# One hybrid decoder step in fp32: the first head's sampled states loaded and used later, and the recurrence's chunks spread differently among the fills

## The chip, the cores and the metric

The kernel runs on one core of a Trainium2 chip. The metric is the device time of the whole launch in microseconds. The kernel before took 1075.98 us as the median of three runs (1078.3, 1072.61 and 1075.98). The engines are named as in the profile: PE (TensorE, matmuls; PEld its weight loads), ACT (ScalarE), DVE (VectorE), POOL (GpSimd) and SP (SyncE), which here issues most of the DMA transfers.

## The reference, cut to what matters

One decoder layer works on 512 prompt tokens and 8 sampled tokens (520 rows in all, width 1024). Two branches start from the same normalised input and the same input projection `w_in`:

```python
s, o = lax.scan(chunk, s0, (split(q), split(k), split(v)))      # retention: 4 heads, key 256, value 512
o = o * lax.rsqrt(jnp.mean(o * o, axis=-1, keepdims=True) + NORM_EPS)
return o * jax.nn.silu(g_a.astype(f32)), s                      # gated by g_a
...
o, s = _rwkv_scan(r, w, k, v, kk, a, s0.astype(f32))            # RWKV-7: 16 heads of 64, a recurrence over tokens
```

Branch A's output (2048 wide) goes through `w_down_a`, branch B's (1024 wide) through `w_down_b`; both are multiplied by merge gates from `w_in` (called MA and MB below), added, and go through `w_out`, a per-layer embedding and a final norm. Prompt tokens start from a zero retention state. Each of the 8 sampled tokens has a state of its own (`state_ret`, 4 heads of 256 x 512 for each token), which is decayed, gets the outer product of the token's key and value added, is multiplied by the query and is written back.

## The kernel before, in words

Each fp32 matmul is made as three fp32r products. `weights` (L144) fetches a block of 1024 x 128 weights into `raw` (SP, L142; three buffers), copies it on ACT to `whi` (L147; two buffers) and takes `wlo = raw - whi` on DVE (L148; two buffers). `mm_half` (L152) then multiplies whi by the high part of the tokens, whi by their low part, and wlo by the high part, for one half of the tokens (256 or 264), into a PSUM bank of tag "h" (four banks). A tile of 1024 x 128 weights is 48 matmuls, a `w_down_a` tile 96.

The program is emitted in one order and then put in order engine by engine by a scheduler that has a time line of its own. What bends it are priorities (`tc.high_priority`), `tc.issue_after(x)`, which lets what follows be placed only behind instruction x, and dependencies added by hand (`after(i, prior)`, L195, a real wait). `tail` holds the last matmul of the last half, `marks` the last weight block's load, subtraction and copy. [...]

The stages: norms and startup; RWKV projections; then the four retention heads. A head makes k and q (L801 to L815), V in four quarters of the weights, j = 0 to 3, into four "h" banks (`phv`, L838; `vsm`, L831, makes the sampled tokens' V from the raw weights), the masked scores (L863 to L868), `sampled(h)` (L748) and four gate tiles (L891, whose sampled part L892 copies to `gs8`). `sampled(h)` loads the head's states in four transfers of 1 MB (POOL, L758; tile tS, four buffers), scales them on ACT (L764, 16 instructions of 512 columns), broadcasts the values (vb, L762), adds on DVE (L765), multiplies with the query (po, L770) and stores them (L774).

Then comes the RWKV recurrence in 8 chunks of 64 tokens. `chunk(c)` (L1017) starts with 64 small matmuls UO (L1025), then copies R, 32 matmuls U (L1034), copies SV, 32 dS (L1040), 32 UO (L1043), and ACT and DVE evacuate (Ot, L1056). Between the parts of a chunk the other engines must answer, and the PE works on fills meanwhile: 8 gate tiles of MB (`gate`, L212; ACT evacuates `mg`, L215) and 8 tiles of `w_down_a` (`down_a`, L1070), in which also the retention outputs are reloaded and split (yalo, yahi; L646). The table AT (L1100) says how many fills have been emitted ahead of each chunk.

Finished rows of the recurrence are stored to DRAM (YBd). Behind the recurrence they are loaded back (yb, L1149, by SP) and split (ybhi on ACT, L1150; yblo on DVE, L1151) for `w_down_b` (`proj`, L152 to L168). The transposes of x and of the embedding (xn, xt, pn, pt; L1157 on) and the loads of MBd and UAd (mb, ma) are placed about there too.

Of the kernel before, what the change touches and what calls it, by code (L numbers as in the profile page):

```python
# [8 lines left out]
F32 = mybir.dt.float32  # L9
F32R = mybir.dt.float32r  # L10
I32 = mybir.dt.int32
AF = mybir.ActivationFunctionType
# [5 lines left out]
T, B8, NT = 512, 8, 520  # L18
# [7 lines left out]
DV = 512  # L26
# [53 lines left out]
def body(tc, A, O, dbg=None, upto="Z"):  # L80
# [3 lines left out]
    act, dve, pe, sp, pool = nc.scalar, nc.vector, nc.tensor, nc.sync, nc.gpsimd  # L84
# [7 lines left out]
    with es:  # L92
# [5 lines left out]
        gs8 = cross.tile([128, 16, B8], F32, tag="gs8", name="gs8")  # L98
# [37 lines left out]
        tail = []  # L136
# [582 lines left out]
        def advance(kind=None):  # L719
            nonlocal due  # L720
            due += LOAD[kind] / UNITS * (WORK + 2 * WAIT) if kind else 2 * WORK
            with tc.issue_after(marks[1]):
                while due > 0:
                    w_ = next(extra, None)
                    if w_ is None:
                        break
                    due -= w_ + 60
# [17 lines left out]
        dve.tensor_tensor(s8, s8, i4[:, 2], ALU.add)  # L745
        dve.tensor_tensor(sum8, s8, i4[:, 3], ALU.add)

        def sampled(h):  # L748
            qz = pR.tile([128, 2, 4, 34], F32, tag="qz", name="qz", bufs=1)
            dve.memset(qz, 0.0)  # L750
            dve.tensor_copy(qz[:, :, :, 0], qs[:, h, :, 0:4])
            dve.tensor_copy(qz[:, :, :, 33], qs[:, h, :, 4:8])
            po = pq.tile([128, 512], F32, tag="po", name="po")
            for g in range(2):
                Ss = []
                for i in range(2):
                    S = pT.tile([128, 4, NT], F32, tag="tS", name="tS", bufs=4)[:, :, 0:DV]
                    pool.dma_start(S, A["state_ret"][0, 4 * g:4 * g + 4, h, 128 * i:128 * i + 128, :].rearrange("b p v -> p b v"))  # L758
                    Ss.append(S)
                for b in range(4):  # L760
                    vb = bank("vb")
                    pe.matmul(vb, sel[:, 4 * g + b, :], vsr, start=True, stop=True)  # L762
                    for i, S in enumerate(Ss):
                        act.activation(S[:, b, :], S[:, b, :], AF.Copy, scale=GAM[h])  # L764
                        last = dve.scalar_tensor_tensor(S[:, b, :], vb, ks[:, h, i, 4 * g + b:4 * g + b + 1], S[:, b, :], ALU.mult, ALU.add)  # L765

                for i, S in enumerate(Ss):
                    n_ = 32 if g == 0 and i == 0 else 2
                    for b in range(4):
                        m_ = pe.matmul(po[32 * b:32 * b + n_, :], qz[:, i, b, 32 * g:32 * g + n_], S[:, b, :],  # L770
                                       start=(n_ == 32), stop=(g == 1 and i == 1), skip_group_check=True)
                        if b == 0 and i == 0:
                            after(m_, last)
                    pool.dma_start(O[5][0, 4 * g:4 * g + 4, h, 128 * i:128 * i + 128, :].rearrange("b p v -> p b v"), S)  # L774
            return po

        def sampled_out(h, po):
# [6 lines left out]
            for i in range(4):  # L784
# [3 lines left out]
                              ps.rearrange("p (i b r) -> p i b r", i=4, b=4)[:, :, :, 0:2],  # L788
                              gs8[:, hs_, :].rearrange("p i (g b) -> p i b g", g=2), ALU.mult)

        OFF = [0, 512, 896, 1152]
        GBC = [0, 0, 0, 4, 8]
        for h in range(H):
# [33 lines left out]
            for j in range(4):  # L827
                ready = fetch(w_in[256 * j:256 * j + 256, O_V + DV * h:O_V + DV * h + DV])
                raws, w = raws[-1:] + [wide(ready[0])], [wide(t) for t in weights(None, ready=ready)]
                if j % 2:  # L830
                    ms = [pe.matmul(vsm[32 * g:32 * g + 32], hst[:, 2 * j - 2 + g, :], raws[g // 2][:, g % 2, :],  # L831
                                    start=(j == 1), stop=(j == 3), skip_group_check=True) for g in range(4)]
                    side_by_side(ms)
                    after(ms[0], marks[2])
                for jt in range(4):
                    for k in range(2):
                        for x, (w_, r) in enumerate(((w[0], hhi), (w[0], hlo), (w[1], hhi))):
                            m_ = pe.matmul(vps[jt], r[:, 2 * j + k, 128 * jt:128 * jt + 128], w_[:, k, :],  # L838
                                           start=(j == 0 and k == 0 and x == 0), stop=(j == 3 and k == 1 and x == 2))
                tail[:] = [getattr(m_, "ins", m_)]  # L840
                advance("v")
            vhi = pB.tile([128, 4, DV], F32R, tag="vhi", name="vhi")
            vlo = pB.tile([128, 4, DV], F32R, tag="vlo", name="vlo")
# [35 lines left out]
            for jt in range(4):  # L879
# [2 lines left out]
                    pe.transpose(ps[:, 128 * i:128 * i + 128], kf[i][:, 128 * jt:128 * jt + 128], ident)  # L882
                act.activation(dhi[:, jt, :], ps[:, 0:256], AF.Copy, scale=kdec[:, h, jt:jt + 1])
                dve.scalar_tensor_tensor(dlo[:, jt, :], ps[:, 0:256], kdec[:, h, jt:jt + 1], dhi[:, jt, :], ALU.mult, ALU.subtract)
            po = sampled(h)

            gs = []
            for i in range(4):
                g = pB.tile([128, NT], F32, tag="vg", name="gs", bufs=4)
                for (j, c0, c1), ps in zip(HV, proj(w_in[:, col(O_GA + DV * h, i)], hhi, hlo)):  # L890
                    act.activation(g[:, c0:c1], ps, AF.Silu)  # L891
                act.activation(gs8[:, 4 * h + i, :], g[:, T:NT], AF.Copy)  # L892
                gs.append(g)
                advance("gate")
                if h == H - 1 and i == 2:
                    ya_tiles(h, pT)
                    ya_load(0, pT, pool)
# [199 lines left out]
            loads(1)  # L1097
        done = []
        nxt_y = beside_rwkv(128, slice(0, 128))
        AT = [0, 3, 6, 8, 9, 11, 12, 13, 16]  # L1100
        for c in range(NCH):
            with tc.high_priority(offset=20000):
                PS = chunk(c)
            if c % 2 == 1:
                x = (Ot, 128, slice((c - 1) * C, (c + 1) * C))
                with tc.high_priority(offset=10000):
                    finish_rwkv(*x)
                done.append((c + 1, x))
            for _ in range(AT[c + 1] - AT[c]):
                next(fl)  # L1110
            if c + 2 < NCH:
                with tc.issue_after(marks[0]), tc.high_priority(offset=20000):
                    loads(c + 2)
            if done and c == done[0][0]:
                with tc.high_priority(offset=10000):
                    emit_rwkv(*done.pop(0)[1], *nxt_y)
                nxt_y = beside_rwkv(128, slice(c * C, c * C + 128)) if c != 4 else beside_rwkv(B8, slice(T, NT))
            if c == 4:
                o8 = pC.tile([128, 16, C], F32, tag="Ot", name="o8", bufs=2)[0:B8]
                pool.dma_start(o8, OSd.rearrange("(b h) v -> b h v", h=16))  # L1120
                x = (o8, B8, slice(T, NT))
                finish_rwkv(*x)
                emit_rwkv(*x, *nxt_y)
                nxt_y = beside_rwkv(128, slice(c * C, c * C + 128))
# [205 lines left out]
```

## Time and profile before

| | us |
|---|---|
| median of three runs | 1075.98 |
| lowest, highest | 1072.61, 1078.3 |
| the profiled execution | 1071.51 |
| its span in the profile | 1069.7 |
| PE busy | 1042.0 (97%) |
| DVE, ACT, POOL busy | 785.2, 494.8, 79.5 |

The profiled execution is 1.81 us longer than its span and 4.47 us below the median. Its mean granted PE clock was 0.992. A profile row gives the start and the duration in us, the engine, the line of the kernel, the operation, what it writes and reads, and in square brackets how long the engine had been idle before it and which instruction's end released it. In a window's row stand, after its bounds and length, each engine's busy time with its number of instructions, the granted clock of PE, the share of the DMA engines and GB/s.

### The profile page before, as it was taken

The page shows a single profiled execution, that of the slowest core. Times are in us where ns is not written, and L with a number is a line of the kernel's source. Part 1 is how long each engine was busy: PE and PEld are TensorE (multiplying, and loading weights), DVE is VectorE, ACT ScalarE, POOL GpSimd, SP SyncE. Part 2 cuts the span into 40 slices and gives each one's busy share as a digit, 9 for nine tenths or more (in the row PEclk, how much of TensorE's full clock was granted, in tenths as well). Part 3 has the DMA queues.
Part 4 walks back from the last instruction along what each step waited for, and adds up shares of the span by engine and source line. Part 5 has one row for each costly group of instructions (what it writes and reads, how often), then busy time and mean ns, then how long its engine had stood idle before and what let it go on. Part 6 is the DMA issues. An engine that isn't in the chain of part 4 may idle for free.

```text
span 1069.7 us, 22049 instructions
## 1 busy us (share of the span) xinstructions
PE 1042.0 (97%) x8932; PEld 974.8 (91%) x8932; DVE 785.2 (73%) x1429; ACT 494.8 (46%) x973; POOL 79.5 (7%) x139
## 2 busy tenths in 40 slices
PE   7999999999999999999999999998999999999995
PEld 6999989999879788987989889898999999999995
DVE  6647989884499699949894698864777755666875
ACT  6744565544464543373445333354323224334554
POOL 2000110100300200010010000110001100000000
PEclk8999999999999999999999999999999999999998
DMA  5623488788943943493288633969996649643222
GB/s 182 179 80 99 122 191 223 188 246 228 330 160 90 327 146 99 144 319 103 86 310 229 230 115 112 328 198 330 309 283 214 171 145 302 206 119 100 81 59 81
DMA packets 239224, 199.45 MB, mean 186 GB/s; under 512 B 58988, under 2 KB 203225, under 8 KB 237970
## 3 DMA queue, kind: packets, MB, share of 16 engines
q1 hardware_dynamic: 225586, 149.60, 47.7%
q0 software_dynamic: 13376, 48.17, 13.2%
q8 instruction: 70, 1.15, 0.4%
q14 instruction: 32, 0.26, 0.1%
q10 hardware_dynamic: 160, 0.27, 0.1%
HBM read 137.70 MB, written 60.00 MB: 185 GB/s over the span
## 4 chain that ended last, share of the span: by engine, by line
PE 85%; DMA 6%; DVE 3%; ACT 2%; issue 1%; SPq 1%; POOL 0%; DVEq 0%; POOLq 0%; ACTq 0%
PE ph L160 58%; PE phv L838 8%; PE o L910 3%; PE st L921 2%; PE sc L863 1%; PE po L770 1%; PE g L506 1%; PE UO L1025 1%; DMA raw<-in_w_ple_gate_dram 1%; DMA raw<-in_w_in_dram 1%; DMA yalo<-YAd 1%; DMA BKt<-BKd 1%; DMA MBd<-mg 1%; PE vb L762 1%; PE vsm L831 1%
## 5 line engine op out<-in xcount | busy, mean ns | idle before, releaser
L160 PE MATMUL ph<-hhi,whi 128*128 128x256 f32 (+2 forms) x1296 | 370.5, 286 | 0.9 <-ACT hhi L282 0.4
L160 PE MATMUL ph<-hlo,whi 128*128 128x256 f32 (+2 forms) x1296 | 369.4, 285 | 0.2 <-DVE hlo L283 0.2
L160 PE MATMUL ph<-hhi,wlo 128*128 128x256 f32 (+2 forms) x1296 | 368.8, 285 | 0.5 <-DVE wlo L148 0.5
L160 PEld LDWEIGHTS ph<-hhi,whi 128*128 128x128 f32 x1296 | 244.2, 189 | 6.1 <-issue 1.7
L160 PEld LDWEIGHTS ph<-hhi,wlo 128*128 128x128 f32 x1296 | 245.0, 189 | 2.2 <-DVE wlo L148 0.7
L160 PEld LDWEIGHTS ph<-hlo,whi 128*128 128x128 f32 x1296 | 244.5, 189 | 1.9 <-DVE hlo L283 0.7
L147 ACT ACTIVATE whi<-raw 128x1024 fp32r<-128x1024 f32 x135 | 142.9, 1059 | 208.9 <-PE ph L160 154.2
L148 DVE TENSOR_TENSOR wlo<-raw,whi 128x1024 fp32r<-128x1024 f32 x135 | 164.8, 1221 | 86.4 <-ACT whi L147 85.4
L160 PE MATMUL ph<-yalo,whi 128*128 128x256 f32 (+1 forms) x256 | 72.4, 285 | 0.0
L160 PE MATMUL ph<-yahi,whi 128*128 128x256 f32 (+1 forms) x256 | 72.2, 284 | 0.0
L160 PE MATMUL ph<-yahi,wlo 128*128 128x256 f32 (+1 forms) x256 | 71.9, 285 | 0.0
L623 DVE TENSOR_TENSOR tm<-M 128x62 f32<-128x62 f32 (+30 forms) x62 | 52.9, 853 | 0.6
L625 DVE TENSOR_TENSOR M<-M,tm 128x62 f32<-128x62 f32 (+30 forms) x62 | 52.8, 852 | 0.6
L838 PE MATMUL phv<-whi,hhi 128*128 128x512 f32 x128 | 51.5, 403 | 0.0
L838 PE MATMUL phv<-whi,hlo 128*128 128x512 f32 x128 | 50.5, 395 | 0.0
L160 PEld LDWEIGHTS ph<-yalo,whi 128*128 128x128 f32 x256 | 48.1, 188 | 0.3
L160 PEld LDWEIGHTS ph<-yahi,whi 128*128 128x128 f32 x256 | 48.1, 188 | 0.2
L160 PEld LDWEIGHTS ph<-yahi,wlo 128*128 128x128 f32 x256 | 47.8, 188 | 0.3
L838 PE MATMUL phv<-wlo,hhi 128*128 128x512 f32 x128 | 46.8, 395 | 0.5 <-DVE wlo L148 0.5
L765 DVE SCALAR_TENSOR_TENSOR tS<-vb,ks,tS 128x512 f32<-128x512 f32 x64 | 44.1, 742 | 3.3 <-PE vb L762 3.3
L764 ACT ACTIVATE tS<-tS 128x512 f32<-128x512 f32 x64 | 35.0, 620 | 12.5 <-DMA tS<-in_state_ret_dram 12.4
L215 ACT ACTIVATE mg<-ph 128x256 f32<-128x256 f32 (+1 forms) x48 | 17.7, 378 | 41.2 <-PE ph L160 20.6
(454 smaller groups left out, 2120.0 us busy)
## 6 DMA issues: line engine op xcount, KB each, us to landing
raw<-in_w_in_dram SPq DMA_DIRECT2D x97, 512.0 KB, 5.0
tS<-in_state_ret_dram POOLq DMA_DIRECT2D x16, 1024.0 KB, 8.4
out_dram<-tS POOLq DMA_DIRECT2D x16, 1024.0 KB, 9.9
KR<-KRd SPq DMA_DIRECT2D x8, 1024.0 KB, 9.5
raw<-in_w_down_a_dram SPq DMA_DIRECT2D x16, 512.0 KB, 6.8
KRd<-KRS SPq DMA_DIRECT2D x16, 256.0 KB, 4.5
KRd<-GM SPq DMA_DIRECT2D x16, 256.0 KB, 4.8
BKt<-BKd SPq DMA_DIRECT2D x8, 512.0 KB, 9.9
```

What stands on the lines that cost most here:

```text
L147: cp = act.activation(hi, raw, AF.Copy)
L148: sb = dve.tensor_tensor(lo, raw, hi, ALU.subtract)
L160: m_ = pe.matmul(ps[:, 0:c1 - c0], w[:, k, :], r[:, k0 + k, c0:c1], start=(x == 0), stop=(x == n_ - 1))
L215: act.activation(g[:, c0:c1], ps, fn, scale=scale)
L506: ms = [pe.matmul(gs[2 * q + hh][:, c * 128:(c + 1) * 128], BK[hs_, 4 * q + c, :], KRS[hs_, 4 * q + c, :], start=True, stop=True) for q in ...
L623: dve.tensor_tensor(tv, M[:, 0:s, s:s + 1].to_broadcast([128, s, n]), M[:, s:s + 1, s + 1:C].to_broadcast([128, s, n]), ALU.mult)
L625: dve.tensor_tensor(M[:, 0:s, s + 1:C], M[:, 0:s, s + 1:C], tv, ALU.add)
L764: act.activation(S[:, b, :], S[:, b, :], AF.Copy, scale=GAM[h])
L765: last = dve.scalar_tensor_tensor(S[:, b, :], vb, ks[:, h, i, 4 * g + b:4 * g + b + 1], S[:, b, :], ALU.mult, ALU.add)
L838: m_ = pe.matmul(vps[jt], r[:, 2 * j + k, 128 * jt:128 * jt + 128], w_[:, k, :], start=(j == 0 and k == 0 and x == 0), stop=(j == 3 and k ...
L910: pe.matmul(ps, a_[:, o_:o_ + 128], b_[:, jt, :], start=(x == 0), stop=(x == len(seq) - 1))
L921: pe.matmul(ps, a_[:, jt, 128 * i:128 * i + 128], b_[:, jt, :], start=(x == 0), stop=(x == 11))
```

## The change

`sampled` is split in two. `sampled_states(h)` asks for the four state transfers; `sampled(h, SS)` uses them. For the first head the transfers wait by a real dependency for the last V matmul of the second quarter (the first two) and of the fourth (the other two), and the use is emitted behind the first gate tile, not ahead of it, and may only be placed behind that tile's copy to gs8. In heads 1 to 3 loads and use are emitted together as before.

In the recurrence the table AT has 6 fills emitted ahead of chunk 1 instead of 3, 8 instead of 6 ahead of chunk 2, 9 instead of 8 ahead of chunk 3, 10 instead of 9 ahead of chunk 4 and the same as before ahead of chunks 5 to 7, and every chunk but the first may only be placed behind the last matmul of the fills emitted so far (`tail[0]`).

```diff
-        def sampled(h):
+        def sampled_states(h):
+            Ss = []
+            for g in range(2):
+                for i in range(2):
+                    S = pT.tile([128, 4, NT], F32, tag="tS", name="tS", bufs=4)[:, :, 0:DV]
+                    ld = pool.dma_start(S, A["state_ret"][0, 4 * g:4 * g + 4, h, 128 * i:128 * i + 128, :].rearrange("b p v -> p b v"))
+                    if h == 0:
+                        after(ld, vmark[g])
+                    Ss.append(S)
+            return Ss
+
+        def sampled(h, SS):
...
             for g in range(2):
-                Ss = []
-                for i in range(2):
-                    S = pT.tile([128, 4, NT], F32, tag="tS", name="tS", bufs=4)[:, :, 0:DV]
-                    pool.dma_start(S, A["state_ret"][0, 4 * g:4 * g + 4, h, 128 * i:128 * i + 128, :].rearrange("b p v -> p b v"))
-                    Ss.append(S)
+                Ss = SS[2 * g:2 * g + 2]
...
+        vmark = []
...
                 tail[:] = [getattr(m_, "ins", m_)]
+                if j % 2:
+                    vmark.append(m_)
                 advance("v")
...
-            po = sampled(h)
+            SS = sampled_states(h)
+            if h:
+                po = sampled(h, SS)
...
-                act.activation(gs8[:, 4 * h + i, :], g[:, T:NT], AF.Copy)
+                a_ = act.activation(gs8[:, 4 * h + i, :], g[:, T:NT], AF.Copy)
                 gs.append(g)
+                if h == 0 and i == 0:
+                    with tc.issue_after(getattr(a_, "ins", a_)):
+                        po = sampled(h, SS)
...
-        AT = [0, 3, 6, 8, 9, 11, 12, 13, 16]
+        AT = [0, 6, 8, 9, 10, 11, 12, 13, 16]
         for c in range(NCH):
-            with tc.high_priority(offset=20000):
+            with ExitStack() as cs_:
+                if c:
+                    cs_.enter_context(tc.issue_after(tail[0]))
+                cs_.enter_context(tc.high_priority(offset=20000))
                 PS = chunk(c)
```

What this moves, at three places. The changed kernel is some lines longer, so that line numbers there are higher (L771 is L764 of before, L903 is L891, L1167 is L1149).

ACT in head 0, from the last evacuation of a k tile (rx) to the third of V's weight copies (L147), before:

```order
L801 ACTIVATE rx<-ph 128x256
L764 ACTIVATE tS<-tS 128x512 x4
L147 ACTIVATE whi<-raw 128x1024
L801 ACTIVATE rx<-ph 128x264
L764 ACTIVATE tS<-tS 128x512 x8
L813 ACTIVATE qhi<-m_3894 128x512
L815 ACTIVATE qs<-m_3894 128x8
L147 ACTIVATE whi<-raw 128x1024
L764 ACTIVATE tS<-tS 128x512 x4
L147 ACTIVATE whi<-raw 128x1024
```

And ACT behind the first gate tile in the changed kernel, where the scalings (tS, now L771) stand; vsr belongs to the sampled values, dhi to the decayed keys, gs and gs_66 to the gates, and the weight copy (L147) at the end is that of gate tile 3, the head's last (they count from 0):

```order
L903 ACTIVATE gs<-ph 128x264
L878 ACTIVATE ihi<-s__4141 128x256
L884 ACTIVATE vsr<-vs 8x512
L904 ACTIVATE gs_66<-gs 128x8
L771 ACTIVATE tS<-tS 128x512 x15
L893 ACTIVATE dhi<-kt,kdec 128x256
L771 ACTIVATE tS<-tS 128x512
L903 ACTIVATE gs<-ph 128x256
L878 ACTIVATE ihi<-s__4152 128x128
L147 ACTIVATE whi<-raw 128x1024
```

The sixteen scalings leave the place among V's weight copies and stand together behind the first gate tile's gs_66, ahead of a weight copy that had none of them in front of it.

PE at the end of chunk 0 and the start of chunk 1 (dS and UO are the recurrence's matmuls, ph those of a fill), before:

```order
L160 MATMUL ph<-hhi,wlo 128x264
L1040 MATMUL dS<-SV,BKt 64x64 x16
L1043 MATMUL UO<-SV,DT 64x64 x16
L1025 MATMUL UO<-SV,KR 64x64 x32
L160 MATMUL ph<-hhi,whi 128x256
L160 MATMUL ph<-hlo,whi 128x256
L1034 MATMUL U<-R,TT 64x64
```

And in the changed kernel:

```order
L160 MATMUL ph<-hhi,wlo 128x264
L1055 MATMUL dS<-SV,BKt 64x64 x16
L1058 MATMUL UO<-SV,DT 64x64 x16
L160 MATMUL ph<-hhi,whi 128x256
L160 MATMUL ph<-hlo,whi 128x256
L160 MATMUL ph<-hhi,wlo 128x256
```

Chunk 1's 64 matmuls UO (printed as 32, two rows of the array side by side) stood directly behind chunk 0; now the 48 of a gate tile come first. The ACT rows around it (yahi, Ot, mg) keep their order. Later chunks stand 96 fill matmuls apart, before 56 to 93.

SP where `w_down_a` ends and `w_down_b` begins, before:

```order
L142 DMA raw<-in_w_down_b_dram 128x8x128
L1074 DMA ua<-MAd 128x520
L142 DMA raw<-in_w_down_b_dram 128x8x128
L1149 DMA yb<-YBd 128x8x128
L1077 DMA UAd<-ua 128x520
L1149 DMA yb<-YBd 128x8x128 x2
L1149 DMA yb<-YBd 128x8x8
L1161 DMA xn<-in_x_prompt_dram 128x512 x2
L1168 DMA pn<-in_p_prompt_dram 128x256
L142 DMA raw<-in_w_down_b_dram 128x8x128 x2
```

And in the changed kernel:

```order
L142 DMA raw<-in_w_down_b_dram 128x8x128
L1089 DMA ua<-MAd 128x520
L142 DMA raw<-in_w_down_b_dram 128x8x128
L1092 DMA UAd<-ua 128x520
L142 DMA raw<-in_w_down_b_dram 128x8x128 x2
L1092 DMA UAd<-ua 128x520
L142 DMA raw<-in_w_down_b_dram 128x8x128
L1167 DMA yb<-YBd 128x8x128 x3
L1167 DMA yb<-YBd 128x8x8
L1179 DMA xn<-in_x_prompt_dram 128x512 x2
```

The four reloads of yb stood behind the second fetch for `w_down_b`; now they stand behind the fifth, and the loads of xn and pn stand behind them as before. On PE, `w_down_b`'s first matmuls (ph from ybhi and yblo) directly follow the last of `w_down_a` in both kernels, but for four transposes xt before.

## The prediction

> **What bounds the kernel now.** I read the page's busy shares first, then the windows of 25 us, and then, in the windows that are not full, what ended TensorE's idle time.
>
> ```profile
> PE 1042.0 (97%) x8932; PEld 974.8 (91%) x8932; DVE 785.2 (73%) x1429; ACT 494.8 (46%) x973; POOL 79.5 (7%) x139
> ```
>
> ```profile
> 275.00:300.00 25.00, 21.83 (x146) 18.70 (x144) 16.03 (x30) 14.97 (x29) 8.31 (x14) 1.00 1.01 381
> 300.00:325.00 25.00, 25.00 (x143) 20.88 (x142) 24.86 (x37) 12.64 (x19) 0.00 (x0) 1.00 0.35 103
> ...
> 725.00:750.00 25.00, 22.27 (x316) 21.12 (x316) 12.68 (x19) 11.04 (x21) 0.00 (x0) 0.93 1.02 328
> 750.00:775.00 25.00, 24.36 (x399) 23.13 (x395) 19.48 (x37) 9.34 (x17) 0.00 (x0) 1.00 1.06 314
> ...
> 875.00:900.00 25.00, 25.00 (x213) 25.00 (x212) 12.96 (x16) 10.95 (x14) 0.85 (x1) 1.00 0.82 234
> ```
>
> The second column is TensorE's busy time. TensorE bounds nearly every stage, and neither kernel has a matmul more or less than the other, so a change of order can only win or lose where TensorE stands still. Those places are few: 3.17 us in head 0 (275 to 300), 2.73 us and 0.64 us at the start of the recurrence (725 to 775). The stretch from 875 to 900 has no idle time; there w_down_a's last tile hands over to w_down_b, and the change goes through it. So there are three places to price: two with a stall to win, one with a full engine that can only lose.
>
> **Place 1, head 0: what is removed.**
>
> ```profile
> 291.91 0.40 PE L838 MATMUL phv<-wlo,hhi 128*128 128x512 f32 x1
> 294.95 1.06 PE L831 MATMUL vsm<-raw,hst 128*32 128x512 f32 x8 [2.64 <-issue]
> ```
>
> ```profile
> 287.78 0.37 ACT L801 ACTIVATE rx<-ph 128x256 f32<-128x256 f32 x1
> 291.71 2.19 ACT L764 ACTIVATE tS<-tS 128x512 f32<-128x512 f32 x4 [3.56 <-DMA tS<-in_state_ret_dram]
> 293.81 1.04 ACT L147 ACTIVATE whi<-raw 128x1024 fp32r<-128x1024 f32 x1
> 294.75 0.37 ACT L801 ACTIVATE rx<-ph 128x264 f32<-128x264 f32 x1
> 295.03 4.26 ACT L764 ACTIVATE tS<-tS 128x512 f32<-128x512 f32 x8
> ```
>
> Four scalings of the sampled states stand on ScalarE ahead of the copy of V's second weight quarter. They wait for their load until 291.71, so the copy begins at 293.81, and TensorE, done with the first quarter at 292.31, stands 2.64 us. Now that copy follows the row at 287.78 directly: 288.15 to 289.2, and the low part some 1.2 us later, both before 292.31. The 2.64 us go: **-2.64**. The other 0.53 us of the 3.17 come before 288.3, from other work, and stay. The window after (300 to 325) has no stall to inherit it, and with the states asked for later the DMA share of 1.01 falls here, so I see nothing else late.
>
> **Place 1: what is added.** The sixteen scalings come back behind the first gate tile's last copy, fifteen in a row, ahead of the weight copy of gate tile 3, the head's last.
>
> ```profile
> 326.46 0.21 ACT L892 ACTIVATE gs<-gs 128x8 f32<-128x8 f32 x1
> 326.58 0.40 ACT L868 ACTIVATE ihi<-s__4141 128x256 fp32r<-128x256 f32 x1
> 327.36 0.59 ACT L874 ACTIVATE vsr<-vs 8x512 fp32r<-8x512 f32 x1 [0.38 <-PE vs L873]
> ...
> 331.50 1.06 ACT L147 ACTIVATE whi<-raw 128x1024 fp32r<-128x1024 f32 x1 [0.61 <-PE ph L160]
> ...
> 337.93 1.06 ACT L147 ACTIVATE whi<-raw 128x1024 fp32r<-128x1024 f32 x1 [2.41 <-PE ph L160]
> ```
>
> Eight took 4.26 us (row at 295.03), so fifteen take 8.0. All times of before now count 2.64 less: the burst starts at 327.95 - 2.64 = 325.3 at the latest, some 324.9 since the copy of vsr moves a little; it ends at about 332.9, and three or four small rows (0.5 and 0.4 each) follow before the copy of gate tile 3, which then begins about 334.4 instead of 328.9 and ends at 335.45, its low part (1.2 us) at 336.7. The copy at 337.93 waited for the end of the tile before, so tile 3's first matmul ran about then; less 2.64, TensorE wants it at 335.3. Its third matmul needs the low part: a new stall of **+1.3**. Bounds: 0, if the burst starts 1.4 us sooner; 3, if the second pair of states (asked for behind the last quarter, landing perhaps 8 us later, about 322) is late. VectorE's updates and TensorE's products with the states follow one another behind the same tile and have the rest of the gate tiles as cover; in head 1 I find no wait that changes. Place 1 is -1.3 in sum.
>
> **Place 2, the second chunk of the recurrence.**
>
> ```profile
> 735.12 2.19 ACT L646 ACTIVATE yahi<-yalo 128x512 fp32r<-128x512 f32 x4 [5.35 <-DMA yalo<-YAd]
> 737.22 0.57 ACT L1056 ACTIVATE Ot<-UO 64x512 f32<-64x512 f32 x1
> 737.70 0.22 ACT L661 ACTIVATE yahi<-yaS 128x32 fp32r<-128x32 f32 x1
> 737.82 0.58 ACT L1056 ACTIVATE Ot<-UO 64x512 f32<-64x512 f32 x1
> 738.29 1.18 ACT L215 ACTIVATE mg<-ph 128x256 f32<-128x256 f32 x4
> ...
> 754.44 0.67 ACT L215 ACTIVATE mg<-ph 128x256 f32<-128x256 f32 x2 [4.31 <-DMA MBd<-mg]
> ```
>
> ```profile
> 737.85 3.59 PE L1025 MATMUL UO<-SV,KR 128*64 128x64 f32 x64 [2.73 <-ACT Ot L1056]
> ...
> 838.91 2.09 PE L1025 MATMUL UO<-SV,KR 128*64 128x64 f32 x64
> ```
>
> ```profile
> 738.00:739.00 1.00, 1.00 (x22) 1.00 (x24) 1.00 (x3) 1.00 (x4) 0.00 (x0) 0.50 1.14 349
> ```
>
> The load of yalo lands late, and four ScalarE rows and two evacuations of UO are queued behind it. TensorE stands 2.73 us, and the granted clock is then 0.50, so that 64 small matmuls take 3.59 us instead of 2.09. The change puts a gate tile (48 matmuls, 0.12 us each by the 213 in the 25 us from 875) ahead of chunk 1 there, which reads as cover. It is none: ScalarE's order is the same, the tile's first matmul needs a PSUM bank that the mg evacuation frees, and that row stands behind both Ot rows. Its first 0.38 us end at 738.67, so TensorE resumes 0.82 us later than the 737.85 of before: **+0.8**. The slow clock falls on the tile instead of the chunk, at the same price. The later wait for MBd<-mg (0.64 us idle in 750 to 775) I leave as it is. From there the chunks stand evenly 96 matmuls (11.5 us) apart; before they had 56 to 93, and nearly nothing was idle, so nothing is to be won. Bounds of the place: -4.2 (stall and slow clock gone, 2.73 + 1.50) to +3.
>
> **Place 3, from w_down_a to w_down_b.** The end of the recurrence moves to a later fill, and SyncE's queue changes: the reloads of yb (L1149), which w_down_b multiplies, stood behind w_down_b's second weight fetch; now they stand behind its fifth.
>
> ```profile
> 884.63 0.37 SPq L142 DMA_DIRECT2D raw<-in_w_down_b_dram  x1
> 885.22 0.41 SPq L1149 DMA_DIRECT2D yb<-YBd  x1
> 885.78 1.17 SPq L1077 DMA_DIRECT2D UAd<-ua  x1
> 887.01 3.63 SPq L1149 DMA_DIRECT2D yb<-YBd  x3
> ```
>
> ```profile
> 890.11 1.06 ACT L1150 ACTIVATE ybhi<-yb 128x1024 fp32r<-128x1024 f32 x1 [3.80 <-DMA yb<-YBd]
> ...
> 892.54 1.06 ACT L1150 ACTIVATE ybhi<-yb 128x1024 fp32r<-128x1024 f32 x1 [0.30 <-DMA yb<-YBd]
> ...
> 896.69 1.06 ACT L147 ACTIVATE whi<-raw 128x1024 fp32r<-128x1024 f32 x1 [0.80 <-PE ph L160]
> ```
>
> ```profile
> 893.64 1.23 DVE L1151 TENSOR_TENSOR yblo<-yb,ybhi 128x1024 fp32r<-128x1024 f32 x1
> ...
> 897.78 1.23 DVE L148 TENSOR_TENSOR wlo<-raw,whi 128x1024 fp32r<-128x1024 f32 x1 [0.31 <-ACT whi L147]
> ```
>
> ```profile
> 896.49 0.28 PE L160 MATMUL ph<-yahi,wlo 128*128 128x264 f32 x1
> ...
> 896.97 0.37 PE L160 MATMUL ph<-ybhi,whi 128*128 128x256 f32 x1
> ```
>
> Before, yblo's second part was ready at 894.87 and w_down_b began at 896.97: 2.1 us to spare. Now count from E, the end of the last w_down_a matmul (896.77 before). The fifth fetch needs the raw buffer of w_down_b's second tile (three buffers), which is free when that tile's low part is made; that needs its high part, and this waits for one of two whi buffers, held until w_down_a's last matmuls. The rows at 896.69 and 897.78 show this very chain: it ends at 899.01, E + 2.24. Only then can SyncE issue the fetch and, 0.59 us behind (884.63 to 885.22), the first yb: E + 2.8. From issue to use that took 4.89 us (885.22 to 890.11): E + 7.7. The first matmul of w_down_b spans two parts of yb; the second part comes between 0.57 us (the next issue, 885.78) and 2.43 us (892.54 - 890.11) later, and I take the middle: E + 9.2. Then ybhi (1.06) to E + 10.3 and yblo (1.23) to E + 11.5, which the second matmul needs. Nothing fills the gap: the transposes of x stand behind w_down_b's first twenty matmuls on TensorE. Stall **+11.4** (10.5 to 12.3), and the slow clock behind it, as at 737.85: **+1.5** (0 to 1.7).
>
> [...]
>
> **The sum**: -2.64 + 1.3 + 0.8 + 11.4 + 1.5 = +12.4. Against the profiled execution's 1071.51 this makes 1083.9; that execution is 4.47 under the median of the runs, and in the median's terms it makes 1088.4.
>
> **Rivals.** (a) The waits in head 0 and in the recurrence both go and yb is in time, as if the fetch of the fifth tile did not hold SyncE's queue: -2.64 - 4.2 = -6.8, 1069, faster. It takes a raw buffer free before E; the rows at 896.69 and 897.78 speak against. (b) The reload is served quicker in queues that are then emptier: if yb needs half of the 4.89 us and its parts land together, the second matmul can run at E + 2.8 + 2.4 + 1.06 + 1.23 = E + 7.5, and with place 2's full gain the sum is -1.3 - 4.2 + 7.5 + 1.5 = +3.5: 1079.5, no difference to be told. For it: the DMA share of 875 to 900 was 0.82, so part of the 4.89 was queueing. (c) The burst on ScalarE costs more than head 0 gains: with 3 us, and the clock halved behind it (1.5), place 1 turns to +1.9 and the sum to 1091.6. For it: no copy on ScalarE overtakes the burst. (d) The even spacing does take away the stall at 735: 1088.4 - 0.8 - 4.2 = 1083.4. Against: mg behind Ot.
>
> **How the numbers follow.** The forecast with (d) 0.76, (c) 0.08, (b) 0.10, (a) 0.06. About 0.5% (5.4 us) is what a measurement of this kernel can tell from no change. Slower by more holds the forecast, (c), (d) and a little of (b): 0.85; within, the rest of (b) and some of (a): 0.09; faster: 0.06. The range reaches down to (b) with 1079.5 and up to 1095, where places 1 and 2 sit at their upper bounds (12.4 + 1.7 + 2.2 = +16.3) and the runs as far above their median as before (2.3).
>
> **What would show it.** Right: one idle stretch of about 11 us on TensorE near 895, ended by yblo or ybhi, and before it yb<-YBd issued directly behind a w_down_b fetch; no 2.64 at 292; a wait of over a microsecond for wlo near 335; a wait of about 3.5 us near 734, ended by mg. Wrong: w_down_b starting without a gap, or a gap under 7 us; a full window at 725 to 750.

## The result, and the profile after

The changed kernel took 1091.39 us as the median of four runs (1088.97 to 1149.26; the last stands far from the other three, whose median is 1089.8, and is not in the ratio), the kernel before 1075.97 us. The ratio is 1.0138, with a 95% interval of 1.0097 to 1.018: slower by about 15 us, where the prediction said 1088 and a range of 1079 to 1095. The profiled execution took 1092.98 us (span 1091.2). That is 21.5 us more than the profiled execution of before, but the one of before stood 4.5 us below its median, so some 15 us are the change and the rest is what executions differ by. Further below, the two are told apart.

The page of the changed kernel, busy shares, and four of its windows, those of the places in the prediction:

```profile
PE 1049.7 (96%) x8932; PEld 978.6 (90%) x8932; DVE 788.3 (72%) x1429; ACT 493.1 (45%) x973; POOL 80.2 (7%) x139
```

```profile
275.00:300.00 25.00, 22.58 (x135) 18.80 (x134) 17.02 (x32) 9.75 (x18) 5.33 (x10) 0.93 0.66 236
...
725.00:750.00 25.00, 20.87 (x266) 20.12 (x265) 12.09 (x19) 9.63 (x19) 0.00 (x0) 0.86 1.01 328
750.00:775.00 25.00, 25.00 (x367) 24.10 (x367) 12.72 (x17) 8.74 (x15) 0.00 (x0) 1.00 1.04 300
...
900.00:925.00 25.00, 12.67 (x83) 12.17 (x82) 9.74 (x15) 8.44 (x14) 0.85 (x1) 0.73 0.80 244
```

TensorE's 8932 instructions are busy 7.7 us longer than before: slow clock, and groups of vsm that are split (below). The window from 900 is new: TensorE works 12.67 of 25 us in it, at a mean clock of 0.73. The stretch from 750 to 775, which lost 0.64 us before, is full. (Two windows of head 3, from 600 to 650, lack 1.18 and 1.02 us, which they did not before; they come up again below.) The timelines of TensorE, ScalarE and SyncE there:

```profile
914.12 0.58 PE L160 MATMUL ph<-ybhi,whi 128*128 128x256 f32 x1 [11.65 <-ACT ybhi L1168]
915.38 0.58 PE L160 MATMUL ph<-yblo,whi 128*128 128x256 f32 x1 [0.68 <-DVE yblo L1169]
```

```profile
902.39 1.06 ACT L147 ACTIVATE whi<-raw 128x1024 fp32r<-128x1024 f32 x1 [1.36 <-PE ph L160]
...
911.31 1.06 ACT L1168 ACTIVATE ybhi<-yb 128x1024 fp32r<-128x1024 f32 x1 [3.64 <-DMA yb<-YBd]
913.01 1.06 ACT L1168 ACTIVATE ybhi<-yb 128x1024 fp32r<-128x1024 f32 x1 [0.65 <-DMA yb<-YBd]
```

```profile
903.48 1.23 DVE L148 TENSOR_TENSOR wlo<-raw,whi 128x1024 fp32r<-128x1024 f32 x1 [0.54 <-ACT whi L147]
```

```profile
904.74 0.37 SPq L142 DMA_DIRECT2D raw<-in_w_down_b_dram  x1
905.32 5.89 SPq L1167 DMA_DIRECT2D yb<-YBd  x4
```

This is the chain of the prediction, step by step. w_down_a ends at 914.12 - 11.65 = 902.47 (E). The weight copy is released there, the low part ends at 904.71, in that moment SyncE issues the fetch, and the first yb follows at E + 2.85. TensorE stands 11.65 us and, after one matmul, 0.68 more.

To see where the rest lies I use the start of ScalarE's weight copies, of which each kernel has 135 in the same order: the 34th (end of the RWKV stage), the 94th (just ahead of the recurrence), the 111th (near the end of w_down_a) and the 121st (inside w_down_b). Every matmul of the recurrence lies between the second and the third of these in each kernel; only its last transposes (gt) stand partly behind the third. Of before, and then of the changed kernel:

```profile
256.00 1.06 ACT L147 ACTIVATE whi<-raw 128x1024 fp32r<-128x1024 f32 x1 [2.35 <-PE ph L160]
...
717.84 1.06 ACT L147 ACTIVATE whi<-raw 128x1024 fp32r<-128x1024 f32 x1 [2.12 <-PE ph L160]
...
872.39 1.06 ACT L147 ACTIVATE whi<-raw 128x1024 fp32r<-128x1024 f32 x1 [1.85 <-PE ph L160]
...
936.92 1.06 ACT L147 ACTIVATE whi<-raw 128x1024 fp32r<-128x1024 f32 x1 [1.50 <-PE ph L160]
```

```profile
254.75 1.06 ACT L147 ACTIVATE whi<-raw 128x1024 fp32r<-128x1024 f32 x1 [0.94 <-PE ph L160]
...
722.98 1.06 ACT L147 ACTIVATE whi<-raw 128x1024 fp32r<-128x1024 f32 x1 [2.12 <-PE ph L160]
...
877.62 1.06 ACT L147 ACTIVATE whi<-raw 128x1024 fp32r<-128x1024 f32 x1
...
958.66 1.06 ACT L147 ACTIVATE whi<-raw 128x1024 fp32r<-128x1024 f32 x1 [1.50 <-PE ph L160]
```

The differences give three stages: heads (before 461.8, after 468.2), recurrence (154.6 and 154.6) and hand-over to w_down_b (64.5 and 81.0). The hand-over lost 16.5 us (0.7 of them are two groups of transposes gt, 0.36 us each, which before stood ahead of the 111th copy) and the recurrence nothing; the heads lost 6.4 us, which the prediction did not have.

### The profile page after: what moved, and what is told of

Same layout as the page of the kernel before. It is cut to its first block, busy times and chain, and to the rows that moved or that the text cites. A ratio compares the mean times of both kernels' runs of the same rounds, so it can differ in the third digit from the quotient of the medians.

```text
span 1091.2 us, 22046 instructions
## 1 busy us (share of the span) xinstructions
PE 1049.7 (96%) x8932; PEld 978.6 (90%) x8932; DVE 788.3 (72%) x1429; ACT 493.1 (45%) x973; POOL 80.2 (7%) x139
## 3 DMA queue, kind: packets, MB, share of 16 engines
q0 software_dynamic: 13376, 48.17, 12.8%
## 4 chain that ended last, share of the span: by engine, by line
PE 81%; DMA 6%; DVE 5%; ACT 3%; SPq 2%; issue 2%; DVEq 0%; POOLq 0%; ACTq 0%
PE ph L160 57%; PE phv L846 6%; PE o L925 3%; PE st L936 2%; PE po L777 1%; PE UO L1040 1%; PE sc L873 1%; DMA raw<-in_w_in_dram 1%; DVE wlo L148 1%; DMA yalo<-YAd 1%; DMA BKt<-BKd 1%; PE g L506 1%; ACT whi L147 1%; PE vb L769 1%; PE vsm L839 1%
## 5 line engine op out<-in xcount | busy, mean ns | idle before, releaser
L147 ACT ACTIVATE whi<-raw 128x1024 fp32r<-128x1024 f32 x135 | 142.9, 1058 | 221.7 <-PE ph L160 147.1
L160 PE MATMUL ph<-yahi,whi 128*128 128x264 f32 (+1 forms) x256 | 73.0, 286 | 0.0
L160 PE MATMUL ph<-yalo,whi 128*128 128x264 f32 (+1 forms) x256 | 72.8, 285 | 0.0
L160 PE MATMUL ph<-ybhi,whi 128*128 128x264 f32 (+1 forms) x128 | 37.7, 294 | 11.7 <-ACT ybhi L1168 11.7
L771 ACT ACTIVATE tS<-tS 128x512 f32<-128x512 f32 x64 | 35.0, 619 | 10.1 <-DMA tS<-in_state_ret_dram 8.4
```

Of the source, the lines that this page charges most:

```text
L147: cp = act.activation(hi, raw, AF.Copy)
L160: m_ = pe.matmul(ps[:, 0:c1 - c0], w[:, k, :], r[:, k0 + k, c0:c1], start=(x == 0), stop=(x == n_ - 1))
```

## The experiments

Each run below was profiled, so that its stages can be set beside these two. The table gives, for each, the three stages in us as worked out above, and the ratio to the kernel before where it was timed. The names of the second, fourth and seventh run do not say what they are: they are further profiles of kernels that had run.

| run | heads | recurrence | hand-over | ratio, 95% interval |
|---|---|---|---|---|
| before | 461.8 | 154.6 | 64.5 | 1 |
| the change | 468.2 | 154.6 | 81.0 | 1.0138 (1.0097 to 1.018) |
| e4, the change, second profile | 465.2 | 153.5 | 81.1 | |
| e1, heads part alone | 466.2 | 161.4 | 65.1 | 1.0017 (0.9994 to 1.004) |
| e2, heads part alone, second profile | 462.0 | 158.6 | 65.0 | |
| e7, heads part alone, third profile | 464.4 | 157.4 | 64.9 | |
| e3, recurrence part alone | 465.7 | 154.6 | 81.1 | 1.0156 (1.0119 to 1.0193) |
| e5, change with the reload ahead | 462.6 | 154.3 | 75.4 | 1.0084 (1.0058 to 1.011) |
| e6, recurrence part, one fill earlier | 467.3 | 155.2 | 69.3 | 1.0026 (1.0004 to 1.0048) |
| e8, e6 with the heads part, vsm together | 463.0 | 154.2 | 69.4 | 1.0019 (0.9997 to 1.004) |
| e9, before, sel first | 467.9 | 158.2 | 64.5 | 1.0016 (0.9996 to 1.0035) |
| e10, heads part, vsm together, sel first | 459.7 | 158.4 | 64.9 | 0.9965 (0.9947 to 0.9982) |
| e11, e8 with the reload ahead | 460.7 | 155.7 | 65.9 | 0.9976 (0.9958 to 0.9993) |
| e12, e11 with sel first | 458.5 | 156.7 | 65.8 | 0.9944 (0.9923 to 0.9966) |

**The two parts apart.** The first kernel has the table and the placing of the chunks as before and only the split of `sampled`:

```diff
-        AT = [0, 6, 8, 9, 10, 11, 12, 13, 16]
+        AT = [0, 3, 6, 8, 9, 11, 12, 13, 16]
...
-            with ExitStack() as cs_:
-                if c:
-                    cs_.enter_context(tc.issue_after(tail[0]))
-                cs_.enter_context(tc.high_priority(offset=20000))
+            with tc.high_priority(offset=20000):
                 PS = chunk(c)
```

The third has the opposite: `sampled` as before, table and placing as changed. Expected of the heads part, its second profile, the recurrence part, and a second profile of the whole change:

> The first part of the change alone (states asked for and used later in head 0); the recurrence as before. Theory A, from the profile after: between the end of the RWKV stage and the first UO of the recurrence TensorE lost 6.4 us against the profile before, of it 1.9 in vsm groups of four that are split into two and two, 1.7 at half clock behind the stall ahead of V's first quarter, and 2.2 in two waits in head 3. Then this is 4 to 6 us slower than before (ratio 1.004 to 1.006). Rival, the prediction's sum for head 0 (-1.3): ratio about 0.999, and the 6.4 us are chance of the one profiled execution.

> The same kernel as in the run before, a second profile of it. Theory A: the split vsm groups (two of 0.98 us each in place of one of 0.99, in heads 1 and 2) are there again, since they are in the order; the half clock behind the stall ahead of V's first quarter may be there or not. Rival: the vsm rows take 0.5 us for each half.

> The second part of the change alone (table and chunks placed behind the fills); the heads as before. Theory: the wait for ybhi ahead of w_down_b is there with 11 to 12 us, some 2 to 4 us of half clock behind it, and 4 us in place of 2.7 at the second chunk: 14 to 17 us slower than before (ratio 1.013 to 1.016). Rival: the wait at w_down_b depends on how late the heads are; then less than 8 us.

> The changed kernel as it is, a second profile. Theory: the wait for ybhi is again 11 to 12 us, since it is a chain that starts at the end of w_down_a, and the losses in the heads that are in the order (split vsm groups) are the same; the clock behind a stall may differ. Rival: the 11.65 us of the first profile hold some chance, and it differs by over 2 us.

The recurrence part alone is 1.0156, the heads part alone 1.0017 with 1 inside its interval: the loss is the recurrence part's, and in it the hand-over. The wait is there again with nearly the same length, TensorE's timeline of the recurrence part alone:

```profile
914.30 0.58 PE L160 MATMUL ph<-ybhi,whi 128*128 128x256 f32 x1 [11.99 <-ACT ybhi L1153]
915.56 0.58 PE L160 MATMUL ph<-yblo,whi 128*128 128x256 f32 x1 [0.68 <-DVE yblo L1154]
```

In the second profile of the change it is 12.19 us. Theory A's 4 to 6 us for the heads fell: the second profile of the heads part took 462.0 us for them, as before. What it lists is of two kinds. One is in the order and in every profile of this part: vsm's groups of four. In head 1, the changed kernel and then a kernel with the group kept together (the eighth run):

```profile
391.86 1.05 PE L839 MATMUL vsm<-raw,hst 128*32 128x512 f32 x4
394.43 1.05 PE L839 MATMUL vsm<-raw,hst 128*32 128x512 f32 x4
```

```profile
391.69 1.06 PE L840 MATMUL vsm<-raw,hst 128*32 128x512 f32 x8
```

Four matmuls of 32 columns (eight records) take 1.06 us when they stand side by side, and two of them take 1.05 us as well. Split in two, this group takes twice the time. The new order put six V matmuls between the halves in heads 1 and 2: 2 x 0.98 = 1.9 us. The other kind is chance: the stall ahead of V's first quarter, which stands in the recurrence part alone, where the heads are those of before,

```profile
290.24 0.50 PE L838 MATMUL phv<-whi,hhi 128*128 128x512 f32 x1 [1.75 <-ACT whi L147]
291.50 0.50 PE L838 MATMUL phv<-wlo,hhi 128*128 128x512 f32 x1 [0.53 <-DVE wlo L148]
298.38 1.06 PE L831 MATMUL vsm<-raw,hst 128*32 128x512 f32 x8 [2.89 <-issue]
```

and is not in the profile of before nor in the second of the heads part. Where it is, the heads take 2.5 to 6.4 us longer with either order; two more waits, of 1.19 and 1.02 us in head 3, stood in the change's first profile and not in its second. Why the stall comes and goes is left open: the loads that it hangs on began up to 2.5 us apart, and the profile does not show what they waited for. The third profile of the heads part was to tell this from the kernel:

> A third profile of the heads part alone. It tells whether the stall of 1.7 to 1.8 us ahead of V's first quarter, with half a clock behind it, which stood in four of six profiles (with both orders of the heads), is a matter of chance: if it is there, the heads take 3.5 to 4.5 us longer than in the profile of before; if not, within 0.5 us of it. Rival: it goes with the kernel; then it stands here as in the first profile of this kernel, and the second was the odd one.

It had the stall (1.75 us) and took 464.4 us, 2.5 us more than before, less than the 3.5 to 4.5 of the expectation: one kernel shows both, so the stall goes with the execution and not with the kernel, and its price was set too high.

**What holds the reload.** The fifth run is the changed kernel with the reload ahead of the fetches, and with w_down_a's last store behind it:

```diff
+        late = []
...
-            sp.dma_start(UAd[m], g)
+            if m < KT - 1:
+                sp.dma_start(UAd[m], g)
+            else:
+                late.append(g)
...
-                sp.dma_start(src, YBd[:, :, cols].rearrange("k r n -> r k n"))
+                ybl = sp.dma_start(src, YBd[:, :, cols].rearrange("k r n -> r k n"))
...
+        with tc.issue_after(getattr(ybl, "ins", ybl)):
+            sp.dma_start(UAd[KT - 1], late[0])
...
-            for (j, c0, c1), ps in zip(HV, proj(A["w_down_b"][0][:, col(0, m)], ybhi, yblo)):
+            with ExitStack() as es_:
+                if m > 1:
+                    es_.enter_context(tc.issue_after(getattr(ybl, "ins", ybl)))
+                pss = proj(A["w_down_b"][0][:, col(0, m)], ybhi, yblo)
+            for (j, c0, c1), ps in zip(HV, pss):
```

> The changed kernel, but SyncE's reloads of yb stand directly behind w_down_b's second fetch, ahead of the other fetches and of w_down_a's last store, which is moved behind them. They then wait only for the recurrence's last matmuls (so), some 2.7 us before the end of w_down_a. Theory (place in SyncE's queue holds the reload): the reload is issued 5 us sooner, the wait for ybhi falls from about 12 to 6 or 7 us, and the time by 5 us or a little more (ratio to before about 1.009 to 1.011 where the change has 1.0138). Rival (the DMA time of the reload is what counts, whatever its place): wait and ratio as in the changed kernel.

The ratio fell from 1.0138 to 1.0084 and the hand-over from 81.0 to 75.4 us. TensorE and SyncE:

```profile
903.39 0.58 PE L160 MATMUL ph<-ybhi,whi 128*128 128x256 f32 x1 [5.36 <-ACT ybhi L1173]
904.65 0.58 PE L160 MATMUL ph<-yblo,whi 128*128 128x256 f32 x1 [0.68 <-DVE yblo L1174]
```

```profile
896.00 4.03 SPq L1172 DMA_DIRECT2D yb<-YBd  x4
900.14 1.91 SPq L1176 DMA_DIRECT2D UAd<-ua  x1
```

The reload is issued at 896.00, 2.03 us ahead of the end of w_down_a (903.39 - 5.36 = 898.03), where the change issued it 2.85 us behind it: 4.9 us sooner, and the wait is 6.3 us shorter. So the place in the queue is shown to be about half of the wait. The other half is that the recurrence itself ends too late: ahead of its last so matmuls the reload cannot go. The sixth run tries that half, the recurrence part with the table `[0, 6, 7, 8, 9, 10, 11, 12, 16]`:

> The recurrence part alone, with the table changed so that chunks 2 to 7 come one fill earlier (0, 6, 7, 8, 9, 10, 11, 12, 16); chunks still stand behind the fills. The last so matmuls then come about 105 fill matmuls ahead of w_down_b instead of 37, and the reload stands behind the third fetch. Theory (the end of the recurrence comes too late for the reload): no wait at w_down_b; and, since the even chunks cost about 0.1 us of waits from the first UO on where three profiles of the old order lost 0, 4 and 7 us more than the first of them, 2 to 4 us faster than before (ratio 0.996 to 0.998). Rival (placing chunks behind the fills costs by itself): 1 us or more slower than before.

The hand-over fell to 69.3 us, with 1.08 us of wait left for ybhi, 1.27 for xn and slow clock behind them. The theory said no wait, and 2 to 4 us faster than before; it is 1.0026. The wait for ybhi all but went, as the theory has it, but the time did not follow; the reload still stood behind one fetch, the third, and the eleventh run below shows that this fetch held it. The eighth run is this recurrence with the heads part repaired:

```diff
-                    ms = [pe.matmul(vsm[32 * g:32 * g + 32], hst[:, 2 * j - 2 + g, :], raws[g // 2][:, g % 2, :],
-                                    start=(j == 1), stop=(j == 3), skip_group_check=True) for g in range(4)]
+                    with tc.high_priority(offset=200):
+                        ms = [pe.matmul(vsm[32 * g:32 * g + 32], hst[:, 2 * j - 2 + g, :], raws[g // 2][:, g % 2, :],
+                                        start=(j == 1), stop=(j == 3), skip_group_check=True) for g in range(4)]
```

> Heads part with vsm's groups of four kept together (a priority on those four matmuls), and the recurrence of the run before (one fill earlier). Theory: 1.9 us from the vsm groups on top of a heads part that is otherwise even with before less 1.7 us, and 2 to 4 us from the recurrence: 4 to 6 us faster than before (ratio 0.9945 to 0.9965). Rival (what the heads win is given back later): no different from the run before.

It gave 1.0019 where 0.9945 to 0.9965 was expected. The heads took 463.0 us although the chance stall stood in its profile, the recurrence 154.2, but the hand-over still cost 4.9 us more than before. With the reload ahead of the third fetch too (the pieces of the fifth run's diff that name ybl, without `late`; w_down_a's last store stays where it is), the eleventh run:

> The changed kernel with three repairs: vsm's groups together, chunks 2 to 7 one fill earlier, and w_down_b's third and later fetches behind the reload of yb in SyncE's queue (sel as before the change). Theory: what was left of the loss at w_down_b with one fill earlier (1.1 us wait for ybhi, 1.4 us for xn, 2 us of half clock) goes, so that the even chunks' gain of about 3 us shows: 3 to 5 us less than with one fill earlier alone (ratio 0.997 to 0.999). Rival: the wait for ybhi stays at about 1 us, for the reload is bound by its own transfer: ratio 1.001 to 1.002.

Now 0.9976. The hand-over is 65.9 us, 1.4 more than before (1.07 us of it a wait for xn), and no wait for ybhi is left.

**The stall ahead of V's first quarter.** It ends when ScalarE has copied the first weights, and ahead of that copy stand ScalarE's copies of sel, which wait for a GpSimd memset queued behind six loads of sv. ScalarE and then GpSimd in the changed kernel, where TensorE stands until 288.11:

```profile
284.23 2.13 ACT L735 ACTIVATE sel<-ident 8x1024 fp32r<-8x1024 f32 x2 [4.43 <-POOL sel L731]
...
287.02 1.04 ACT L147 ACTIVATE whi<-raw 128x1024 fp32r<-128x1024 f32 x1
```

```profile
280.05 3.18 POOL L668 DMA_DIRECT2D sv<-SMd  x6 [25.19 <-DMA raw<-in_w_in_dram]
283.22 0.97 POOL L731 MEMSET sel<- 128x1024 f32 x1
```

The ninth run moves the loads behind the memsets, in the kernel before:

```diff
-        for i in range(6):
-            pool.dma_start(sv[:, i, :], SMd[i].rearrange("b (h k) -> (b h) k", k=C))
...
+        for i in range(6):
+            pool.dma_start(sv[:, i, :], SMd[i].rearrange("b (h k) -> (b h) k", k=C))
         hst = pR.tile([128, KT, 32], F32, tag="hst", name="hst")
```

> The kernel before, with GpSimd's six loads of sv moved behind the memsets of sel and vsr in its queue. In eight of ten profiles so far TensorE stood 0.6 to 1.8 us ahead of V's first quarter, because ScalarE's copies of sel, which wait for GpSimd's memset behind the sv loads, stand ahead of that quarter's weight copy; half a clock followed. Theory: the stall and the half clock go in every execution, 2 to 3.5 us where they stood: 1.5 to 3 us faster than before (ratio 0.997 to 0.9985). Rival: the weights' own arrival holds the copy; then the stall stays and the time is the same.

TensorE's idle time in it:

```profile
289.67 0.50 PE L838 MATMUL phv<-wlo,hhi 128*128 128x512 f32 x1 [0.68 <-DVE wlo L148]
298.41 1.93 PE L831 MATMUL vsm<-raw,hst 128*32 128x512 f32 x8 [4.76 <-issue]
```

```profile
295.18 2.19 ACT L764 ACTIVATE tS<-tS 128x512 f32<-128x512 f32 x4 [5.67 <-DMA tS<-in_state_ret_dram]
```

The stall for whi is gone, here and in the tenth and the last run, which have the same edit (but it was also absent in three of the eleven profiles without it). Still the ratio is 1.0016, no gain. The wait behind the first quarter, in which ScalarE (second fence) waits for the states, is 4.76 us in place of 2.64 to 3.69. Counted from the 34th copy, TensorE came to it 0.7 us sooner than in the recurrence part alone, and the states, of which three loads were issued only at 288.84, landed 1.1 us later than there. So what was freed in the first stall was waited for in the second. With the states taken out of the way (the tenth run: heads part, vsm together, sel first, the recurrence of before) the same edit could pay:

> Heads part of the change with vsm's groups of four kept together, and sel ahead of sv as in the run before; the recurrence as before the change. Theory: the 1.7 us that the heads part wins in head 0 are kept, since the 1.9 us of the split groups are gone: 1.5 to 2 us less than the run before (ratio 0.995 to 0.997). Rival (the burst of sixteen scalings eats it): no difference from the run before.

0.9965, as expected: the heads took 459.7 us, 2.1 less than in the best profile of the old order. Against the ninth run this is 5.5 us by the ratios and not 1.5 to 2; the wait of 4.76 us for the states, which the ninth run has, is not there. The last run puts all repairs together:

> All repairs in one kernel: heads part with vsm's groups together and sel ahead of sv, chunks 2 to 7 one fill earlier, w_down_b's third and later fetches behind the reload of yb. Theory (the terms add): the repaired heads alone are 0.9965 of before, and the repaired recurrence took about 3 us less than the old order took in most profiles but returned 1 us for xn: 1 to 2 us less than the repaired heads alone, ratio 0.9945 to 0.996. Rival (the old recurrence's waits are chance that the median does not hold): ratio 0.9965 to 0.998.

0.9944, with an interval of 0.9923 to 0.9966: 6 us faster than the kernel before and, by the two ratios, some 21 us faster than the change. The ratio is at the good end of what adding the repairs gave, but that they add up is not shown: its interval overlaps that of the tenth run, and the two kernels' own medians are 1072.71 and 1071.46 us. The kernel before took 1079.21 us beside the last run and 1076.33 beside the tenth, and the lower ratio comes from there. For the same reason the gain of sel first by itself (0.9944 against 0.9976 in the eleventh run, again with overlapping intervals) is not shown. One wait for mg of 4.34 us at the second chunk and 0.87 us for xn are what is left of the places in this text:

```profile
737.66 0.58 PE L160 MATMUL ph<-hhi,whi 128*128 128x256 f32 x1 [4.34 <-ACT mg L215]
...
898.73 0.66 PE L1183 MATMUL xt<-ident,xn 128*128 128x128 f32 x4 [0.87 <-DMA xn<-in_x_prompt_dram]
```

## Why the prediction was right, and where it was not

**Place 3** decided, as forecast, by the chain that was forecast: E + 2.24 for the low part (2.24 measured), E + 2.8 for the issue (2.85). Two terms were too small. From issue to use it was 5.99 us (905.32 to 911.31) where 4.89 was taken from the row of before, so that the stall is 12.3 us and not 11.4. And the slow clock lasted longer. One-microsecond windows of the changed kernel behind the stall:

```profile
916.00:917.00 1.00, 1.00 (x6) 1.00 (x6) 0.82 (x1) 0.29 (x2) 0.00 (x0) 0.50 1.03 359
...
919.00:920.00 1.00, 1.00 (x6) 1.00 (x6) 0.00 (x0) 0.00 (x0) 0.00 (x0) 0.50 0.96 377
920.00:921.00 1.00, 1.00 (x8) 1.00 (x7) 0.00 (x0) 0.30 (x1) 0.00 (x0) 0.64 0.28 111
```

TensorE worked at 0.50 from 914.1 to about 920.7 (0.64 is 0.72 us at half speed in the last window), 6.6 us, and not the 3.4 us behind the stall of before at 737.85; it cost about 3 us where 1.5 was put in. No run shows the 1.7 us that the forecast had as the upper end of this cost; what the changed kernel shows is 6.6 us at 0.50, in which TensorE stood for 0.68 us, so that half of the other 5.9, some 3 us, was lost. The whole place cost 16.5 us by the stages where 12.9 was forecast, 0.7 of them for the transposes gt.

**Place 1**: the 2.64 us are gone in every profile with the states moved, and the burst is where it was put: at 323.32 in the second profile of the heads part, which lacks the stall ahead of V's first quarter (68.7 us behind the 34th copy, 68.9 to 69.3 forecast), and later by about that stall in the changed kernel. ScalarE's burst and TensorE's stall there:

```profile
327.04 7.91 ACT L771 ACTIVATE tS<-tS 128x512 f32<-128x512 f32 x15
```

```profile
338.55 0.38 PE L160 MATMUL ph<-hhi,wlo 128*128 128x256 f32 x1 [0.18 <-DVE wlo L148]
```

The new stall is 0.18 us and not 1.3. The low part came 0.9 us behind the tile's first matmul, where 1.4 was forecast, and four matmuls that need no low part stand at the head of the last gate tile, not two. What failed is the sentence "in head 1 I find no wait that changes": no wait did, but the groups of vsm were split there and in head 2, 1.9 us that the order shows and that I had not looked for. So the heads part alone came out near zero (1.0017) where -1.3 was summed.

**Place 2**: right in kind, TensorE waits for mg in place of Ot:

```profile
744.39 0.58 PE L160 MATMUL ph<-hhi,whi 128*128 128x256 f32 x1 [4.13 <-ACT mg L215]
```

The wait was forecast at 3.5 us; it is 4.13 here, 2.73 in the second profile of the change, and 2.7 to 5.2 in all profiles with the new placing. "At the same price" did not hold for the slow clock: in the changed kernel it lasted 6.8 us behind this wait (743.2 to 750.0), in the one of before 3.4 us (737.8 to 741.2). What failed besides is "nearly nothing was idle, so nothing is to be won" by the even spacing. That was read from one execution in which the recurrence took 154.6 us. Five more of the old order took 157.4 to 161.4, with waits for Ot, R and SV at changing places, the first profile of the heads part for one:

```profile
745.52 3.74 PE L1040 MATMUL UO<-SV,KR 128*64 128x64 f32 x64 [5.07 <-ACT Ot L1071]
...
766.74 3.48 PE L1040 MATMUL UO<-SV,KR 128*64 128x64 f32 x63 [3.82 <-ACT Ot L1071]
```

The new order took 153.5 to 154.6 in four profiles. The mean of the old six is 158.1, so by the profiles the even chunks win some 4 us, 0.7 us of it at most for transposes gt that moved into the next stage. The hand-over takes this back four times over. The timed runs do not confirm the size: four of the five later profiles of the old order stood 1 to 7 us above their kernel's median, and the recurrence part alone was 16.8 us slower (12.8 to 20.8) where the stages give 16.6 - 4 = 12.6. That the sum (+12.4) came near the measured 15 us is in part luck: place 3 cost 3.6 us more than was put in and the split groups 1.9 us, and against them stands what the even chunks won.

Of the rivals, (b) (the reload served quicker in emptier queues) fell: it was slower, 5.99 us. (a) needed a raw buffer free before E, and the rows of the changed kernel show it was not. (c) did not occur; (d) neither.

## What to carry to other kernels

When a chunked recurrence is dealt further apart among its cover, look at what its end feeds: here the last reload fell behind weight fetches that wait for buffers of the work in front, and that place in the queue made about half of the wait, the late end of the chain the rest. Move the end of such a chain only as far as its reload still fits ahead of the stage that uses it, and give the reload its place in the queue by hand. And read gains of waits from several profiles: one execution may be the lucky one. And before a stall is removed, look at the next one: if that waits for something which does not come sooner, it takes up what was freed.

## What was not expected of the hardware

In these profiles the length of a stall does not tell how long the half clock (0.50 in the windows) behind it lasts. It was 3.4 us behind the stall of 2.73 us at 737.85 in the profile of before, 6.8 us behind the one of 4.13 us in the changed kernel; in the eleventh run, behind one of 5.23 us, the fills' matmuls began 0.21 us apart in place of 0.12 from 739.7 to 742.5, some 3 us. Stalls of 2.64 us (before, at 292) and 2.88 us (tenth run, at 736) brought none: all windows from 290 to 298 are at 1.00 in the one, and the 64 matmuls UO took 2.13 us in the other, against 2.09 at full clock and 3.59 at half in the profile of before. And 1.73 and 0.53 us, one shortly after the other (changed kernel, at 288), brought 3.4 us, while behind 1.75 and 0.53 us (recurrence part alone, at 290) V's matmuls began 0.23 us apart up to 295, as at full clock in the changed kernel; at half clock they began 0.43 us apart there. At the hand-over of the changed kernel the clock fell while TensorE still stood:

```profile
906.00:907.00 1.00, 0.00 (x0) 0.00 (x0) 0.00 (x0) 0.00 (x0) 0.00 (x0) 1.00 0.62 146
907.00:908.00 1.00, 0.00 (x0) 0.00 (x0) 0.21 (x2) 0.31 (x1) 0.00 (x0) 0.53 0.95 255
```

So it was at half from 907.06 (0.53 is 0.94 us at half speed) to 920.72, 13.66 us, of which TensorE worked in the last 6.6. By such windows the half clock lasted 3.42 us in the profile of before (737.78 to 741.20), and in the changed kernel 3.42 (289.24 to 292.66), 6.82 (743.22 to 750.04) and 13.66 us: the longer two are two and four times the shortest. What sets these lengths is not shown.

In the changed kernel two of the vsm matmuls of 32 columns took 1.05 us (at 391.86, and the other two at 394.43), as long as the four that followed each other directly in the eighth run (1.06 us, at 391.69).
